# Hybrid attention, S5 and PEER block on one core: gather steps handed out between the dense blocks, GELU as one ScalarE operation

## The chip, the core and the metric

The kernel runs on one core of a Trainium2 chip. The metric is the device time of one execution in microseconds (us), the median of several runs. The engines are TensorE (PE; PEld is its weight load), VectorE (DVE), ScalarE (ACT), GpSimd (POOL), which issues the indirect gathers here, and SyncE (SP), which issues most other transfers. Sixteen DMA engines move the data.

## The reference

One block of a diffusion backbone works on 1024 latent tokens of width 1024 with 256 context tokens: attention and a state-space branch, merged by gates and projected, then PEER retrieval, then the output. All is in float32. The part that matters here is the last one, PEER: for each token eight heads choose 16 of 16384 single-neuron experts each, so 128 rows of `peer_u` and 128 rows of `peer_v`.

```python
def retrieve(xb):                       # one block of 128 tokens
    ...                                 # top-k of product keys -> experts, top_s
    g = jax.nn.softmax(top_s, axis=-1).astype(xb.dtype)
    act = jax.nn.gelu(jnp.einsum('thkd,td->thk', u_tab[experts], xb))
    return jnp.einsum('thk,thkd->td', g * act, v_tab[experts])
```

`jax.nn.gelu` is the tanh form: 0.5 x (1 + tanh(c2 x (1 + c1 x^2))).

## The kernel before

The 1024 tokens are eight tiles of 128. They go through the front part (attention, gates, projection, routing) in four groups: tile 0; 1 and 2; 3, 4 and 5; 6 and 7. `route` chooses the experts of a group. The retrieval is then done in two ways.

**By gathers** (tiles 0, 1, and 6, 7, the list `VEC`). `score` takes 128 steps per tile: in a step GpSimd gathers one row of `peer_u` per token (tile `ub`, 128 x 1024, L1274), and DVE multiplies it with the tile's input and sums to one dot product (L1278). `weighted` then applies the GELU and the gate to the 128 x 128 dot products and takes another 128 steps: a gather of `peer_v` rows (`vb`, L1316) and one DVE step that adds the weighted row to the sum `f` (L1319). All gathered rows share six buffers. `retrieve` interleaves the two: the weighted steps of one tile stand between the scoring steps of the next. For tiles 6 and 7 that is 512 gathers.

**Over all experts** (tiles 2 to 5, the list `DENSE`, 512 tokens at once). `dense` goes through the 16384 experts in 128 blocks of 128, two to a turn of its loop. A block loads its part of `peer_u` (transposed) and `peer_v` and splits each into a high and a low part (`u`, `v`: a cast on ACT and a subtraction on DVE of 1024 columns, L232 and L233). 24 matmuls of 512 columns (L1233 to L1235) give the dot products of all 512 tokens in one bank, `turn`. The GELU and a product with `gt`, which holds each token's gate for the experts of the block and zero elsewhere (spread out earlier from `pl` by `spread`), follow in 128 x 512 tiles `x` and `act`. The result is split into `kpe_h` and `kpe_l`, and 24 more matmuls (L1194 to L1196) add high and low products to the sums `fd` of four tiles by two halves. Seven of those eight sums have a bank of their own. The last, the "aside", has none: its three matmuls write to `turn`, from where ACT copies them (`more`, L1201) and DVE adds them to `rest` (L1202). In the code the values of a block come after the `turn` matmuls of the next (`late`).

The program is emitted in one order of code, with priorities, and a scheduler then fixes the order of the instructions of each engine at build time; each engine runs its own list in that order. The last lines of `block_kernel` are where the two ways meet: the first pairs of blocks are emitted between steps of the last group's routing, then `retrieve(VEC)` emits all 512 gather steps, and after it come the remaining pairs of blocks. What is emitted earlier has the better place where both are ready. The GELU of a block before is

```python
                S.copy(x, turn)
                S.activation(w, x, func=AF.Square, scale=math.sqrt(GC1))
                V.scalar_tensor_tensor(w, w, 1.0, x, op0=ADD, op1=MUL)
                xc = x.rearrange("p (c t) -> p c t", t=CHUNK)
                V.tensor_tensor(xc, xc, gt[:, :, 2 * (p % GTP) + c, :], op=MUL)
                S.activation(w, w, func=AF.Tanh, scale=GC2)
                V.scalar_tensor_tensor(w, w, 1.0, x, op0=ADD, op1=MUL)
```

where `S` is ACT and `V` is DVE. These are L1238 to L1244.

## Time and profile before

| what | value |
| --- | --- |
| time, median of 3 runs | 3889.87 us (3882.73 to 3898.87) |
| profiled execution | 3890.37 us, of which the profile's span is 3888.6 us |
| PE busy, share of the span | 3431.8 us, 88% |
| DVE busy | 3037.1 us, 78% |
| ACT busy | 1645.2 us, 42% |
| POOL busy | 1443.5 us, 37% |
| moved by DMA | 1032.55 MB, 266 GB/s on the mean |
| mean granted clock of PE | 0.936 |

The span is one execution as the hardware profiler saw it. Busy times are unions of what the engine's instructions cover; matmuls are pipelined, so the duration of one overlaps the next, and the pace is better read from how many of them fall in a stretch. The granted clock is the share of TensorE's full clock that it got. A wait is put down to the engine and line that released it last. Shares over the whole span mix the front part with the stage over all experts; the stretches below are cut from that stage.

### The profile page before, as it was taken

How to read it: one execution, taken by the hardware profiler on the slowest of the kernel's cores; microseconds unless marked ns; L12 is line 12 of the kernel's file. 1: busy time of each engine (PE TensorE's matmuls, PEld its weight loads, DVE VectorE, ACT ScalarE, POOL GpSimd, SP SyncE). 2: the span in 40 equal slices, each digit the busy share in tenths (PEclk: the TensorE clock that was granted, in tenths of full speed). 3: DMA queues.
4: the chain of work that ended last, by engine and by line, in shares of the span. 5: the costliest groups of instructions: out<-in, count | busy, mean ns of one | idle time of the engine just before them, and what ended most of it. 6: DMA issues, size and time to landing. Idle time of an engine off the chain costs nothing.

```text
span 3888.6 us, 55690 instructions
## 1 busy us (share of the span) xinstructions
PE 3431.8 (88%) x20022; PEld 2769.1 (71%) x20022; DVE 3037.1 (78%) x7128; ACT 1645.2 (42%) x3216; POOL 1443.5 (37%) x1254
## 2 busy tenths in 40 slices
PE   5978888879779899799999798899889999999997
PEld 3745577878656688576687687677667777777885
DVE  7368656775898776889566688999999999998556
ACT  2223363441323564133498953334333344444442
POOL 5045300040554633543522102765666653442000
PEclk7988899999889999899999899899999999999998
DMA  8742375494897899978877655999999998897331
GB/s 281 223 83 71 128 268 193 159 358 167 312 347 271 313 346 339 341 280 285 309 286 310 263 179 197 353 352 336 343 350 359 345 349 297 311 336 273 115 124 71
DMA packets 348725, 1032.55 MB, mean 266 GB/s; under 512 B 46592, under 2 KB 142080, under 8 KB 322592
## 3 DMA queue, kind: packets, MB, share of 16 engines
q0 software_dynamic: 147456, 536.94, 37.8%
q1 hardware_dynamic: 164032, 462.20, 33.6%
q10 hardware_dynamic: 36960, 29.86, 2.4%
q8 instruction: 157, 2.57, 0.3%
q14 instruction: 120, 0.98, 0.1%
HBM read 961.27 MB, written 67.62 MB: 265 GB/s over the span
## 4 chain that ended last, share of the span: by engine, by line
PE 43%; issue 12%; DVE 12%; DMA 8%; ACT 5%; POOL 5%; another core or an unknown queue 0%; SPq 0%; DVEq 0%; POOLq 0%; ACTq 0%
DMA ub<-in_peer_u,ei 4%; PE turn L1234 4%; PE turn L1233 4%; POOL ub L1274 4%; PE turn L1235 4%; DVE ub L1278 4%; PE fd L1195 4%; PE fd L1196 4%; PE fd L1194 3%; PE acc L1354 2%; PE pe L1151 2%; PE pqr L1065 2%; PE po L808 2%; ACT first L1147 1%; DMA vb<-in_peer_v,eiT 1%
## 5 line engine op out<-in xcount | busy, mean ns | idle before, releaser
L1274 POOL DMA_INDIRECT ub<-in_peer_u,ei x512 | 649.2, 1268 | 1130.8 <-DVE ub L1278 350.7
L1278 DVE SCALAR_TENSOR_TENSOR ub<-ub,h 128x1024 f32<-128x1024 f32 x512 | 617.2, 1220 | 64.3 <-DMA ub<-in_peer_u,ei 55.0
L1316 POOL DMA_INDIRECT vb<-in_peer_v,ei x256 | 327.4, 1279 | 316.6 <-DVE f L1319 257.3
L1349 POOL DMA_INDIRECT vb<-in_peer_v,eiT x256 | 281.3, 1099 | 415.3 <-PE acc L1354 318.4
L1195 PE MATMUL fd<-v,kpe_l 128*128 128x512 f32 x891 | 366.8, 412 | 44.4 <-DVE kpe_l L233 44.3
L1233 PE MATMUL turn<-hh,u 128*128 128x512 f32 x1024 | 401.1, 392 | 0.2 <-ACT x L1238 0.2
L1234 PE MATMUL turn<-hh,u 128*128 128x512 f32 x1024 | 400.7, 391 | 0.1
L1235 PE MATMUL turn<-hl,u 128*128 128x512 f32 x1024 | 399.3, 390 | 0.0
L1194 PE MATMUL fd<-v,kpe_h 128*128 128x512 f32 x891 | 341.7, 404 | 35.5 <-ACT kpe_h L232 35.3
L1196 PE MATMUL fd<-v,kpe_h 128*128 128x512 f32 x891 | 359.8, 404 | 0.0
L1319 DVE SCALAR_TENSOR_TENSOR f<-vb,zz,f 128x1024 f32<-128x1024 f32 x254 | 325.3, 1281 | 4.9 <-DMA vb<-in_peer_v,ei 3.8
L233 DVE TENSOR_TENSOR u<-w,u 128x1024 fp32r<-128x1024 f32 x128 | 157.9, 1234 | 116.2 <-ACT u L232 112.7
L1195 PEld LDWEIGHTS fd<-v,kpe_l 128*128 128x128 f32 x891 | 173.5, 195 | 91.4 <-DVE kpe_l L233 52.6
L1194 PEld LDWEIGHTS fd<-v,kpe_h 128*128 128x128 f32 x891 | 170.6, 193 | 84.9 <-ACT kpe_h L232 43.3
L1233 PEld LDWEIGHTS turn<-hh,u 128*128 128x128 f32 x1024 | 192.2, 188 | 43.5 <-ACT x L1238 0.4
L1235 PEld LDWEIGHTS turn<-hl,u 128*128 128x128 f32 x1024 | 192.3, 188 | 41.9
L1234 PEld LDWEIGHTS turn<-hh,u 128*128 128x128 f32 x1024 | 192.2, 188 | 40.8 <-DVE u L233 0.5
L1238 ACT COPY x<-turn 128x512 f32<-128x512 f32 x128 | 75.0, 586 | 316.4 <-PE turn L1235 316.3
L232 ACT CAST v<-w 128x1024 fp32r<-128x1024 f32 x128 | 134.6, 1052 | 167.7 <-PE fd L1195 163.1
L1354 PE MATMUL acc<-vb,diag 128*32 128x256 f32 x2048 | 163.1, 399 | 46.7 <-DMA vb<-in_peer_v,eiT 42.2
L1148 DVE TENSOR_SCALAR second<-iota,pl 128x128 f32<-128x128 f32 x512 | 141.5, 350 | 79.4 <-PE pe L1151 65.6
L1196 PEld LDWEIGHTS fd<-v,kpe_h 128*128 128x128 f32 x891 | 173.3, 194 | 40.8
(422 smaller groups left out, 8623.7 us busy)
## 6 DMA issues: line engine op xcount, KB each, us to landing
w<-in_peer_uT SPq DMA_DIRECT2D x64, 1024.0 KB
w<-in_peer_v SPq DMA_DIRECT2D x64, 1024.0 KB
w<-in_peer_wq SPq DMA_DIRECT2D x32, 1024.0 KB
gT_d<-stage SPq DMA_DIRECT2D x16, 2048.0 KB
gt<-gT_d SPq DMA_DIRECT2D x32, 1024.0 KB
vh<-v_d SPq DMA_DIRECT2D x32, 640.0 KB
w<-k_d SPq DMA_DIRECT2D x32, 640.0 KB
w<-in_w_mod_b SPq DMA_DIRECT2D x16, 1024.0 KB
```

What stands on the lines that cost most here:

```text
L1194: PE.matmul(o, ah[:, ts], vh[:, cs], start=first, stop=False)
L1195: PE.matmul(o, al[:, ts], vh[:, cs], start=False, stop=False)
L1196: return PE.matmul(o, ah[:, ts], vl[:, cs], start=False, stop=final)
L1233: PE.matmul(turn, uh[:, k, :], hh[:, k, :], start=(k == 0), stop=False)
L1234: PE.matmul(turn, ul[:, k, :], hh[:, k, :], start=False, stop=False)
L1235: PE.matmul(turn, uh[:, k, :], hl[:, k, :], start=False, stop=(k == 7))
L1274: GP.indirect_dma_start(out=ub, out_offset=None, in_=a["peer_u"], in_offset=bass.IndirectOffsetOnAxis(ap=ei[:, s:s + 1], axis=0))
L1278: V.scalar_tensor_tensor(ub, ub, 1.0, h2, op0=MUL, op1=MUL, accum_out=dots[:, s:s + 1])
L1316: GP.indirect_dma_start(out=vb, out_offset=None, in_=a["peer_v"], in_offset=bass.IndirectOffsetOnAxis(ap=ei[:, s:s + 1], axis=0))
L1319: V.scalar_tensor_tensor(f, vb, z[:, s:s + 1], f, op0=MUL, op1=ADD)
L1349: GP.indirect_dma_start(out=vb, out_offset=None, in_=a["peer_v"], in_offset=bass.IndirectOffsetOnAxis(ap=eiT[:, t:t + 1], axis=0))
L1354: PE.matmul(acc[d // 2][o:o + 32, 256 * (d % 2):256 * (d % 2) + 256], dg[:, q, jj, :], vb[:, d * 256:(d + 1) * 256], start=False, stop=Fal ...
```

## The change

Three things change. In a block of `dense`, one ACT operation, `Gelu_apprx_tanh`, reads the bank `turn` and writes `act`, which now has two buffers; the copy `x`, the square, the tanh and two of the three DVE steps are gone. The factor 0.5 that the gates `pl` carried is gone too, since this GELU has it. In `weighted`, the tiles 6 and 7 use the same ACT operation; tiles 0 and 1 keep the old form. And `retrieve` is a generator now: the remaining pairs of blocks are emitted first in each turn of a loop, and eight steps of `retrieve(VEC)` after each pair, until the steps run out.

```diff
-                    S.mul(pl[:, 2], pt[:, 1, :], 0.5)
+                    S.copy(pl[:, 2], pt[:, 1, :])
...
-                x = N.tile([128, ntok], F32, tag="x", name="x")
-                w = N.tile([128, ntok], F32, tag="act", name="act")
-                S.copy(x, turn)
-                S.activation(w, x, func=AF.Square, scale=math.sqrt(GC1))
-                V.scalar_tensor_tensor(w, w, 1.0, x, op0=ADD, op1=MUL)
-                xc = x.rearrange("p (c t) -> p c t", t=CHUNK)
-                V.tensor_tensor(xc, xc, gt[:, :, 2 * (p % GTP) + c, :], op=MUL)
-                S.activation(w, w, func=AF.Tanh, scale=GC2)
-                V.scalar_tensor_tensor(w, w, 1.0, x, op0=ADD, op1=MUL)
+                w = N.tile([128, ntok], F32, tag="act", bufs=2, name="act")
+                S.activation(w, turn, func=AF.Gelu_apprx_tanh)
+                wc = w.rearrange("p (c t) -> p c t", t=CHUNK)
+                V.tensor_tensor(wc, wc, gt[:, :, 2 * (p % GTP) + c, :], op=MUL)
...
             for s, _ in enumerate(score(l, ei, dots)):
                 if n and s % n == 0:
                     next(before, None)
+                yield
             for _ in before:
-                pass
+                yield
             before = weighted(l, ei, eiT, g, dots)
         for _ in before:
-            pass
+            yield
...
+        if l in VEC:
+            S.activation(z, dots, func=AF.Gelu_apprx_tanh)
+            V.tensor_tensor(z, z, g, op=MUL)
+        else:
...
-    retrieve(VEC)
-    with tc.high_priority(offset=PDENSE):
-        for _ in tokens:
-            pass
+    beside = retrieve(VEC)
+    for _ in tokens:
+        for _ in range(PACE):
+            next(beside, None)
+    for _ in beside:
+        pass
```

`PACE` is 8, `tokens` is the generator of `dense` (one pair of blocks a step). Below, lines after the change are a few numbers lower or higher: the scoring step L1278 is L1273, the product with the gates L1242 is L1239, and the new GELU is L1237.

**DVE in the scoring of tile 6**, one block from gate product to gate product. Before:

```order
L1244 SCALAR_TENSOR_TENSOR act<-act,x 128x512
L1278 SCALAR_TENSOR_TENSOR ub,dots<-ub,h_22240 128x1024 x2
L233 TENSOR_TENSOR v<-w,v 128x1024
L233 TENSOR_TENSOR kpe_l<-act,kpe_h 128x512
L1278 SCALAR_TENSOR_TENSOR ub,dots<-ub,h_22240 128x1024 x4
L233 TENSOR_TENSOR u<-w,u 128x1024
L1240 SCALAR_TENSOR_TENSOR act<-act,x 128x512
L1202 TENSOR_TENSOR rest<-rest,more 128x512
L1278 SCALAR_TENSOR_TENSOR ub,dots<-ub,h_22240 128x1024 x2
L1242 TENSOR_TENSOR x<-x,gt 128x512
```

After, in the same stretch:

```order
L233 TENSOR_TENSOR u<-w,u 128x1024
L1273 SCALAR_TENSOR_TENSOR ub,dots<-ub,h_22343 128x1024
L1202 TENSOR_TENSOR rest<-rest,more 128x512
L233 TENSOR_TENSOR kpe_l<-act,kpe_h 128x512
L1273 SCALAR_TENSOR_TENSOR ub,dots<-ub,h_22343 128x1024 x2
L233 TENSOR_TENSOR v<-w,v 128x1024
L1273 SCALAR_TENSOR_TENSOR ub,dots<-ub,h_22343 128x1024 x2
L1239 TENSOR_TENSOR act<-act,gt 128x512
```

Two of the five steps of 512 columns are gone from the block, and five scoring steps stand in it where eight stood; over the whole stretch the mean was 6.7 and is 4.8. Counted over the lists, the 512 gather steps of tiles 6 and 7 lay on blocks 9 to 102 and now lie on blocks 9 to 119 (blocks are counted from 0).

**PE between two `turn` groups**, where the aside writes to `turn`. Before, as in 53 of the 127 blocks:

```order
L1235 MATMUL turn<-hl,u 128x512
L1194 MATMUL fd<-v,kpe_h 128x512 x2
L1194 MATMUL turn<-v,kpe_h 128x512
L1195 MATMUL fd<-v,kpe_l 128x512
L1196 MATMUL fd<-v,kpe_h 128x512
```

After, as in 57 of them, the end of one block's values and the `turn` group of the next:

```order
L1194 MATMUL fd<-v,kpe_h 128x512
L1195 MATMUL fd<-v,kpe_l 128x512
L1196 MATMUL fd<-v,kpe_h 128x512
L1194 MATMUL fd<-v,kpe_h 128x512 x2
L1233 MATMUL turn<-hh,u 128x512
...
L1235 MATMUL turn<-hl,u 128x512
L1195 MATMUL fd<-v,kpe_l 128x512
L1196 MATMUL fd<-v,kpe_h 128x512
L1195 MATMUL fd<-v,kpe_l 128x512
L1196 MATMUL fd<-v,kpe_h 128x512
L1194 MATMUL turn<-v,kpe_h 128x512
```

In these blocks the first two products with `kpe_h` moved ahead of the next block's `turn` group, and four matmuls instead of two stand between that group and the aside; in most of the other blocks six do, as in most of the others before.

**ACT beside the last routing**, after the change (`g` is the softmax of a tile's gates; `qh` and `sc` are copies of the routing). Before, the same place has no table load:

```order
L1069 COPY qh<-pqr 128x256
L1038 ACTIVATE g<-g 128x64
L1237 ACT_TABLE_LOAD
L1237 ACTIVATE act<-turn 128x512
L232 CAST u<-w 128x1024
L1074 COPY sc<-pz 128x256
L1038 ACT_TABLE_LOAD
L1038 ACTIVATE g<-g 128x64
```

Seven such loads are new, all in this stretch; the lists have ten after and three before.

## Rows read from the trace of the kernel before

**Rows 1.** Page, busy tenths in 40 slices: TensorE, and its granted clock in tenths.
```profile
PE   5978888879779899799999798899889999999997
...
PEclk7988899999889999899999899899999999999998
```

**Rows 2.** Stretches: us; PE, PEld, DVE, ACT, POOL busy (instructions); clock, DMA share, GB/s.
```profile
2390.00:3842.00 1452.00, 1362.99 (x5689) 1082.77 (x5688) 1270.42 (x1662) 582.41 (x832) 678.14 (x511) 0.97 0.82 295
3580.00:3842.00 262.00, 262.00 (x1136) 212.95 (x1135) 133.39 (x178) 113.56 (x165) 0.00 (x0) 1.00 0.35 117
2390.00:2660.00 270.00, 232.57 (x933) 182.34 (x932) 256.05 (x404) 95.82 (x137) 185.55 (x130) 0.92 0.94 343
2745.00:3130.00 385.00, 341.38 (x1376) 266.27 (x1375) 372.44 (x510) 140.71 (x201) 254.20 (x187) 0.95 0.95 350
3270.00:3550.00 280.00, 276.59 (x1185) 220.99 (x1183) 268.55 (x285) 121.83 (x173) 133.03 (x112) 1.00 0.92 327
```

**Rows 3.** Waits of TensorE from 2390 to 2660 us: us in total, times, longest.
```profile
PE fd L1194 <- ACT kpe_h L232: 20.2, 6, 11.0
PE fd L1195 <- DVE kpe_l L233: 16.1, 8, 3.5
```

**Rows 4.** The same from 2745 to 3130 us.
```profile
PE fd L1195 <- DVE kpe_l L233: 26.2, 14, 4.0
PE fd L1194 <- ACT kpe_h L232: 15.1, 8, 3.3
```

**Rows 5.** VectorE in order of time near 2600 us: start, us, instruction.
```profile
2600.53 0.68 DVE L1244 SCALAR_TENSOR_TENSOR act<-act,x 128x512 f32<-128x512 f32 x1
2601.13 1.21 DVE L233 TENSOR_TENSOR v<-w,v 128x1024 fp32r<-128x1024 f32 x1
2602.27 1.21 DVE L1278 SCALAR_TENSOR_TENSOR ub<-ub,h 128x1024 f32<-128x1024 f32 x1
...
2603.41 0.68 DVE L233 TENSOR_TENSOR kpe_l<-act,kpe_h 128x512 fp32r<-128x512 f32 x1
```

**Rows 6.** The same near 3350 us, weighted steps.
```profile
3350.78 1.27 DVE L1319 SCALAR_TENSOR_TENSOR f<-vb,zz,f 128x1024 f32<-128x1024 f32 x1
3351.97 0.68 DVE L1244 SCALAR_TENSOR_TENSOR act<-act,x 128x512 f32<-128x512 f32 x1
```

**Rows 7.** VectorE's groups from 2745 to 3130 us: xcount, busy us, mean ns.
```profile
L1278 DVE SCALAR_TENSOR_TENSOR ub<-ub,h 128x1024 f32<-128x1024 f32 x123 | 148.2, 1219 | 5.9 <-DMA ub<-in_peer_u,ei 5.6 <-issue 0.2
L1319 DVE SCALAR_TENSOR_TENSOR f<-vb,zz,f 128x1024 f32<-128x1024 f32 x64 | 82.2, 1285 | 3.9 <-DMA vb<-in_peer_v,ei 3.5 <-DVE rest L1202 0.3
```

**Rows 8.** ScalarE's groups by form, whole span: xcount, busy us, mean ns.
```profile
L871 ACT ACTIVATE P<-pS,mb 128x512 f32<-128x512 f32 x128 | 87.0, 686 | 108.2 <-DVE mb L866 95.9 <-DVE mb L865 8.0 <-DVE eiT L1108 2.2
L1239 ACT ACTIVATE act<-x 128x512 f32<-128x512 f32 x128 | 81.0, 633 | 48.6 <-DVE kpe_l L233 48.5
...
L232 ACT CAST kpe_h<-act 128x512 fp32r<-128x512 f32 x128 | 79.3, 620 | 165.3 <-DVE act L1244 165.2
...
L1238 ACT COPY x<-turn 128x512 f32<-128x512 f32 x128 | 75.0, 586 | 316.4 <-PE turn L1235 316.3
...
L629 ACT ACT_TABLE_LOAD x1 | 1.3, 1283 | 0.4 <-ACT vt L698 0.4
```

**Rows 9.** Waits of TensorE from 3300 to 3540 us.
```profile
PE turn L1194 <- ACT x L1238: 2.9, 11, 0.3
```

**Rows 10.** DMA from 2390 to 3580 us: packets, MB, share; one issue row.
```profile
q0 software_dynamic: 73728, 268.47, 61.5%
q1 hardware_dynamic: 69431, 128.42, 30.8%
...
w<-in_peer_v SPq DMA_DIRECT2D x47, 1024.0 KB
```

**Rows 11.** Waits of VectorE from 2390 to 3580 us.
```profile
DVE ub L1278 <- DMA ub<-in_peer_u,ei: 15.5, 21, 1.8
...
DVE f L1319 <- DMA vb<-in_peer_v,ei: 3.8, 6, 1.0
```

More of the change, by code (lines that the diff above doesn't have):

```diff
@@ L69 @@
 PRIO = (0, 1500, 1500, 3000, 2000)
-PDENSE = 0
+PACE = 8
 RAT = 3
@@ L1305, in weighted @@
         z = pp.tile([128, 128], F32, tag="zz", name="zz")
-        V.tensor_tensor(z, dots, dots, op=MUL)
-        V.tensor_scalar(z, z, GC1, 1.0, op0=MUL, op1=ADD)
-        V.tensor_tensor(z, z, dots, op=MUL)
-        S.activation(z, z, func=AF.Tanh, scale=GC2)
-        V.scalar_tensor_tensor(z, z, 1.0, dots, op0=ADD, op1=MUL)
-        V.scalar_tensor_tensor(z, z, 0.5, g, op0=MUL, op1=MUL)
+        if l in VEC:
+            S.activation(z, dots, func=AF.Gelu_apprx_tanh)
+            V.tensor_tensor(z, z, g, op=MUL)
+        else:
+            V.tensor_tensor(z, dots, dots, op=MUL)
+            V.tensor_scalar(z, z, GC1, 1.0, op0=MUL, op1=ADD)
+            V.tensor_tensor(z, z, dots, op=MUL)
+            S.activation(z, z, func=AF.Tanh, scale=GC2)
+            V.scalar_tensor_tensor(z, z, 1.0, dots, op0=ADD, op1=MUL)
+            V.scalar_tensor_tensor(z, z, 0.5, g, op0=MUL, op1=MUL)
         if l in VEC:
@@ L1468, in block_kernel @@
         if gi == RAT:
-            retrieve([l for l in range(NL) if l not in DENSE + VEC])
+            for _ in retrieve([l for l in range(NL) if l not in DENSE + VEC]):
+                pass
     with tc.high_priority(offset=PRIO[-1]):
@@ L1484, in block_kernel @@
     turns[1] = 1
-    retrieve(VEC)
-    with tc.high_priority(offset=PDENSE):
-        for _ in tokens:
-            pass
+    beside = retrieve(VEC)
[3 more added lines that the diff above has]
+    for _ in beside:
+        pass
     psum.release()
```

## The prediction

> **What bounds the kernel now.** I read the page's slices first. The change acts only where the stage over all experts runs, from slice 23 or 24 on (a slice is 97.2 us), since the order of every engine is the same up to its first block. There TensorE (PE) is busy 8 or 9 tenths of nearly every slice and its clock is at or near full, with dips on the way [rows 1]. So the question is how much of that stage is PE work and how much is PE waiting.
>
> The table of stretches answers it. A block of the stage is 48 matmuls of 512 columns. From 3580 to 3842 us no gather runs any more, PE is busy for all 262 us at clock 1.00 and does 1136 matmuls: 262 / 1136 = 0.2306 us each, 11.07 us for a block [rows 2]. I take that as PE's own pace. From 2390 to 3842 us it did 5689 matmuls, which at that pace take 1312 us; they took 1452. So **140 us** of this stage are lost, and nothing that speeds up the other engines can win back more. Where: 270 - 933 x 0.2306 = 55 us from 2390 to 2660, 385 - 1376 x 0.2306 = 68 us from 2745 to 3130, and only 280 - 1185 x 0.2306 = 7 us from 3270 to 3550 [rows 2]. In the two bad stretches the granted clock was 0.92 and 0.95 on the mean, so part of the loss is the clock that fell after PE had idled; the idle itself is 270 - 233 = 37 and 385 - 341 = 44 us.
>
> The waits of PE name the releaser: fd L1194 and L1195 wait for kpe_h and kpe_l, the two halves of the activations, 20.2 + 16.1 us and 15.1 + 26.2 us [rows 3, 4]. These come out of the GELU chain, most of which stands in the queue of VectorE (DVE), and DVE is busy 256 of 270 and 372 of 385 us there [rows 2].
>
> Is it DVE's own work? The spacing of starts in the timeline gives what an instruction takes from the queue: 0.60 us for 512 columns, 1.14 for a split of 1024 or for one scoring step, 1.19 for one weighted step [rows 5, 6]. A block of before has two splits of 1024 and five of 512 columns (L1240, L1242, L1244, kpe_l, rest): 2 x 1.14 + 5 x 0.60 = 5.28 us. From 2745 to 3130 us that is 1376 / 48 = 28.7 blocks x 5.28 = 151, plus 123 x 1.14 = 140 for scoring and 64 x 1.19 = 76 for weighting [rows 7], together 367 of 385 us. So DVE set the pace there, at 13.4 us a block. From 3270 to 3550 us 112 gathers fell on 24.7 blocks, 4.5 a block, DVE needed 5.28 + 4.5 x 1.19 = 10.7 us, less than 11.07, and PE was bound by itself. The bound is thus **DVE where more than about 4.8 gathers fall on a block, and PE elsewhere**.
>
> **The change part by part.**
>
> *The GELU.* Per block it takes L1240 and L1244 off DVE (2 x 0.60 us) and the copy, the square and the tanh off ScalarE (ACT; rows of 586 and 633 ns [rows 8]) and adds one ACT operation from PSUM. DVE's share of a block falls from 5.28 to 4.08 us. The new operation isn't in the trace; its bounds are the PSUM copy of the same tile, 586 ns, and the exponential from PSUM of the same size, 686 ns [rows 8]; I take 640, nearest to the tanh of 633. Either way it is hidden: ACT has over half its time free. It also holds the bank "turn" as the copy did, so the next user, the aside's first L1194, must wait for it. In the order of before two matmuls often stand ahead of that one and it waits, at most 0.3 us a time [rows 9]; in the new order at least four stand ahead in nearly every block (0.92 us), which covers 0.69 and a semaphore. If the operation took over 1 us that cover would be gone.
>
> *Table loads.* The new order has seven more ACT_TABLE_LOADs, all beside the route of the last group, where GELU and the Exp of L1038 alternate; after that none. One took 1283 ns [rows 8]: 9.0 us on ACT, spread over the blocks in which PE has the route's matmuls to do as well. Between 0 (all covered) and 9 us I take 4, because a load just ahead of a GELU also delays the release of "turn".
> The Trainium skill (ScalarE: Activation LUTs, "Table sets: the hidden batching unit") says to batch activations by table set rather than by function, which speaks against this change, and prices a load at some 2.7 us; by that the term would be up to 19 us. This case's row has about half that price, so the row decides, and the built order shows that only seven alternations are left.
>
> *The gather steps.* All 512 of the last two token tiles stay; they move. Before, they had the better place in the queue and sat at 6.7 and 6.5 a block in the scoring stretches, ending 25 blocks before the end. Now they lie over blocks 9 to 119, 4.6 a block, densest 4.8 (blocks 9 to 35). DVE then needs 4.08 + 4.6 x 1.17 = 9.5 us of each 11.07, 85%; in the densest 9.6. So DVE no longer sets the pace and **the waits for kpe_h and kpe_l should go**. With PE not idling I also expect the clock rows to stay at 1.00, as they do from 3270 on.
>
> *What is late next: DMA.* The gathers' queue took 61.5% of 1190 us for 511 gathers, 1.43 us each, and the loads' queue 30.8% for 47 pairs of blocks, 3.9 us a block [rows 2, 10]. The new mix asks for 4.6 x 1.43 + 3.9 = 10.5 us in 11.07, a share of 0.95; the densest part 10.8, 0.97. A share of 0.92 went together with PE at full pace (3270 to 3550), and 0.95 was held for 385 us [rows 2], with DVE waiting for gathers only 15.5 + 3.8 us in the whole stretch to 3580 [rows 11]. So it fits, narrowly. If 0.95 is the most that it holds, the 27 dense blocks take 10.8 / 0.95 = 11.35 us, 8 us in all. Each gather on GpSimd's queue waits only for a free row buffer; the loads stand on SP's queue in the old sequence, the loads of the two tile ends now later in it.
>
> *The rest.* The 0.5 that leaves the copy of the gates costs nothing (same copy, same size). The tail after 3842 us is PE and the settling of four tiles, unchanged.
>
> **Sum**, against the profiled run (3890.4 us, span 3888.6; the median of the runs is 3889.9, so no correction): -140 if PE never waits. Added back: 4 for table loads, 8 for DMA, and 12 for small waits: at 4.5 gathers a block the loss was 7 in 280 us, 2.5%, and since the aside's part of it should go I take 1% of the 111 x 11.07 = 1229 us. 3890.4 - 140 + 24 = **3774 us**. Its own range is 3750 (no loss at all) to 3788.
>
> **The rivals.**
>
> *DMA becomes the bound.* For it: the share of 0.95 is the highest that any long stretch shows, and gathers now run nearly to the end, so no slack is left behind them. Against: DVE's waits for gathers were small even there. If only 0.92 or 0.90 can be used, blocks take (1.43 x gathers + 3.9) / share: over the four parts of the gather stretch (4.81, 4.57, 4.63 and 4.44 a block, 27, 7, 41 and 36 blocks) that adds 37 or 65 us to 3890.4 - 140 + 4: **3791 to 3819 us**.
>
> *A new wait for kpe_h.* In some 57 blocks the new order puts the first two L1194 of a block's values ahead of the next block's "turn" matmuls, so kpe_h is wanted 24 x 0.2306 = 5.5 us after "turn" ends, not 11. The chain is 0.69 (GELU) + 0.60 (gate product) + 0.62 (kpe_h [rows 8]) = 1.9 us, plus what DVE has in hand: three scoring steps still fit (5.3), a fourth or a gather that is late (longest 1.8 us [rows 11]) does not. At 1 to 2 us for each of 57 blocks, on top of the forecast: **3831 to 3888 us**, the upper end no change.
>
> *Slower: the gathers set the end.* All gathers share six row buffers, and one late gather holds everything behind it on DVE, the gate product and the splits included. If thinner spacing made a gather cost more than 2.7 us, the last would land after 2390 + 512 x 2.7 = 3772, then 8 blocks (89) and the tail (47) give 3908, and from there on the kernel is slower. At 2.9 us it is **4010 us**. Against: a gather cost 385 / 187 = 2.06 us when pushed and 2.5 us when the order spaced it [rows 2]; the plan asks for 2.4.
>
> *It doesn't do what it says.* If the GELU operation took 1.5 us or more from PSUM, the aside would wait some 0.7 us in each block, 85 us: about **3860 us**. No row comes near that duration.
>
> **How the numbers follow.** Forecast (3750 to 3788) 0.60; DMA as the bound 0.22; the new wait for kpe_h 0.08 (a quarter of it within 0.5% of now, which is about what a measurement of this kernel can tell from no change); slower 0.05; a slow GELU 0.05 (half of it within 0.5%). Faster by over 0.5%, that is below 3870: 0.60 + 0.22 + 0.06 + 0.02 = 0.90; within: 0.05; slower: 0.05. The range for 8 in 10 runs from 3748 to 3822: it takes in the forecast and the DMA case to its dearer end.
>
> **What would show it.** Right: in the stretches of the gathers some 173 matmuls in 40 us, clock 1.00, DVE about 85% busy, no wait of PE for kpe_h or kpe_l above a few us in total, a GELU row of about 0.64 us, DMA at 0.93 to 0.96, gathers ending some 90 us before the last block. Wrong: DVE idle in front of the scoring and weighted steps, released by the gathers' DMA (DMA bound); PE idle before fd L1194 released by kpe_h although DVE has time free (new wait); PE idle before turn L1194 in every block (slow GELU). The prediction fails altogether if PE's pace of 0.2306 us, taken where DMA ran at a share of 0.35, can't be held beside gathers.

## The result and the profile after

The changed kernel takes 3759.27 us (median of 4 runs, 3758.54 to 3767.63) beside 3888.99 us for the kernel before on the same chip (4 runs): a ratio of 0.9669, 95% interval 0.9651 to 0.9687. The profiled execution took 3758.8 us, its span 3757.0: 131.6 us less than the profiled one of before.

The page's slices of the kernel after, TensorE and its granted clock, to be read beside [rows 1]:

```profile
PE   5968888979779889879989879999999999999997
...
PEclk7978999989889989989999989999999999999998
```

The first 24 slices are much like before; from slice 25 (a slice is 93.9 us now) PE is at 9 in all but the last, and the clock with it. The stretches of the stage, with the columns of [rows 2]:

```profile
2390.00:2430.00 40.00, 37.89 (x162) 29.81 (x161) 35.33 (x59) 12.93 (x18) 25.05 (x18) 1.00 0.83 296
2430.00:2510.00 80.00, 78.10 (x331) 62.84 (x330) 70.56 (x107) 24.62 (x34) 50.19 (x37) 0.98 0.98 367
2510.00:2670.00 160.00, 160.00 (x694) 129.47 (x693) 140.09 (x209) 54.00 (x75) 91.78 (x68) 1.00 0.94 336
2745.00:3130.00 385.00, 385.00 (x1668) 312.07 (x1667) 335.38 (x434) 126.73 (x172) 215.87 (x161) 1.00 0.94 341
3160.00:3540.00 380.00, 380.00 (x1646) 306.95 (x1645) 337.93 (x365) 124.22 (x171) 215.89 (x152) 1.00 0.93 335
```

Where before did 1376 matmuls in the 385 us from 2745 on, after does 1668, one every 0.2308 us; DVE fell from 372 to 335 us busy (87%), and DMA from 0.95 to 0.94 although the stage goes faster. Of the waits of PE, those on kpe_h [rows 3, 4] are gone and those on kpe_l nearly so. From 2390 to 3700 us all that is left of PE's waits is:

```profile
PE fd L1195 <- DVE kpe_l L233: 3.6, 3, 1.7
PE turn L1194 <- ACT act L1237: 0.4, 2, 0.2
```

The GELU and the table loads, ScalarE's groups by form (xcount, busy us, mean ns, idle before), beside [rows 8]:

```profile
L1237 ACT ACTIVATE act<-turn 128x512 f32<-128x512 f32 x128 | 76.6, 598 | 588.0 <-PE turn L1235 587.9
...
L1237 ACT ACT_TABLE_LOAD x4 | 5.1, 1283 | 0.1
...
L1038 ACT ACT_TABLE_LOAD x3 | 3.8, 1283 | 0.1
```

For the comparisons below two measures are worked out from the order in time of ScalarE and VectorE, the same way for each kernel. **Block 9 to 127** is the time from the start of block 9's first ScalarE operation on `turn` to that of block 127; 118 blocks at 11.07 us are 1306 us. It leaves out the front part, which differs between profiled runs (block 9 began at 2384 us in one and at 2416 in another, with the same work ahead of it). **The chain** of a block runs from that same start to the end of its kpe_l. Both are from one profiled execution of each kernel. The six kernels in which gather steps and blocks are tied to each other (explained below) take 45 us from the start of block 127 to their end, before and after 39; those 6 us go with the ties.

| kernel | gather steps per block while scoring | ratio to before (95%) | block 9 to 127, us | chain in blocks 42 to 83: mean (longest), us |
| --- | --- | --- | --- | --- |
| before | 6.5 to 6.7 | 1 | 1446.5 | 11.7 (16.9) |
| after | 4.6 to 4.8 | 0.9669 (0.9651 to 0.9687) | 1315.7 | 4.8 (6.0) |
| new GELU alone | as after | 0.9659 (0.9612 to 0.9706) | 1313.5 | 4.8 (6.0) |
| hand-out alone | as before | 1.001 (0.9988 to 1.0033) | 1450.5 | 11.7 (17.3) |
| old GELU, spread steps | as after | 0.9987 (0.9966 to 1.0008) | 1436.0 | 13.1 (16.9) |
| the same, steps behind kpe_l | as after | 0.9887 (0.9864 to 0.991) | 1391.4 | 11.2 (16.6) |
| new GELU, dense steps | as before | 0.9963 (0.9946 to 0.998) | 1430.5 | 9.7 (22.3) |
| the same, steps behind kpe_l | as before | 0.9989 (0.9971 to 1.0006) | 1440.5 | 9.6 (18.8) |
| the same, half rows | as before | 0.9823 (0.9798 to 0.9847) | 1368.0 | 7.7 (15.2) |
| after + 2 DVE operations beside | 5.5 to 5.6 | 0.9792 (0.977 to 0.9815) | 1369.4 | 10.4 (16.8) |
| after + 4 ACT operations in the chain | 4.6 to 4.9 | 0.9662 (0.9645 to 0.968) | 1323.0 | 7.5 (9.8) |
| after + 8 ACT operations in the chain | 4.7 to 5.1 | 0.9717 (0.9694 to 0.974) | 1332.2 | 10.4 (11.8) |
| after + a write of 0.5 MB per pair | as after | 0.9812 (0.9778 to 0.9846) | 1365.8 | 9.0 (19.7) |

So before lost 140 us against 1306 between these two blocks, and after loses 9. Seven of the nine lie in blocks 10 to 12, the first behind the last routing, whose chains take 10.6 to 15.6 us.

### The profile page after: what moved, and what is told of

Read it like the earlier page. It is cut to its first block, busy times and chain, and to the rows that moved or that the text cites. A ratio compares the mean times of both kernels' runs of the same rounds, so it can differ in the third digit from the quotient of the medians.

```text
span 3757.0 us, 54909 instructions
## 1 busy us (share of the span) xinstructions
PE 3376.1 (90%) x20022; PEld 2741.5 (73%) x20022; DVE 2889.2 (77%) x6864; ACT 1496.5 (40%) x2967; POOL 1477.3 (39%) x1254
## 4 chain that ended last, share of the span: by engine, by line
PE 56%; DVE 9%; issue 7%; DMA 5%; ACT 4%; POOL 2%; SPq 0%; DVEq 0%; ACTq 0%; POOLq 0%
PE turn L1233 6%; PE turn L1234 6%; PE turn L1235 6%; PE fd L1194 5%; PE fd L1195 5%; PE fd L1196 5%; DMA ub<-in_peer_u,ei 2%; PE pqr L1065 2%; DVE ub L1273 2%; PE acc L1354 2%; PE pe L1151 2%; DMA vb<-in_peer_v,eiT 2%; PE po L808 2%; PE po L953 1%; POOL ub L1269 1%
## 5 line engine op out<-in xcount | busy, mean ns | idle before, releaser
L1269 POOL DMA_INDIRECT ub<-in_peer_u,ei x512 | 639.6, 1249 | 1221.7 <-DVE ub L1273 446.8
L1273 DVE SCALAR_TENSOR_TENSOR ub<-ub,h 128x1024 f32<-128x1024 f32 x512 | 617.0, 1219 | 52.4 <-DMA ub<-in_peer_u,ei 46.5
L1316 POOL DMA_INDIRECT vb<-in_peer_v,ei x256 | 363.4, 1420 | 266.3 <-DVE f L1319 203.6
L1195 PE MATMUL fd<-v,kpe_l 128*128 128x512 f32 x891 | 353.5, 397 | 3.6 <-DVE kpe_l L233 3.6
L1196 PE MATMUL fd<-v,kpe_h 128*128 128x512 f32 x891 | 351.1, 394 | 0.0
L1194 PE MATMUL fd<-v,kpe_h 128*128 128x512 f32 x891 | 341.5, 397 | 0.0
L1237 ACT ACTIVATE act<-turn 128x512 f32<-128x512 f32 x128 | 76.6, 598 | 588.0 <-PE turn L1235 587.9
L1196 PEld LDWEIGHTS fd<-v,kpe_h 128*128 128x128 f32 x891 | 167.6, 188 | 41.5
L1194 PEld LDWEIGHTS fd<-v,kpe_h 128*128 128x128 f32 x891 | 167.3, 188 | 40.7
L233 DVE TENSOR_TENSOR v<-w,v 128x1024 fp32r<-128x1024 f32 x128 | 156.6, 1223 | 43.4 <-ACT v L232 42.7
```

What stands on the lines that cost most here:

```text
L1194: PE.matmul(o, ah[:, ts], vh[:, cs], start=first, stop=False)
L1195: PE.matmul(o, al[:, ts], vh[:, cs], start=False, stop=False)
L1196: return PE.matmul(o, ah[:, ts], vl[:, cs], start=False, stop=final)
L1269: GP.indirect_dma_start(out=ub, out_offset=None, in_=a["peer_u"], in_offset=bass.IndirectOffsetOnAxis(ap=ei[:, s:s + 1], axis=0))
L1273: V.scalar_tensor_tensor(ub, ub, 1.0, h2, op0=MUL, op1=MUL, accum_out=dots[:, s:s + 1])
L1316: GP.indirect_dma_start(out=vb, out_offset=None, in_=a["peer_v"], in_offset=bass.IndirectOffsetOnAxis(ap=ei[:, s:s + 1], axis=0))
```

## The experiments

### Which part of the change did it

Two kernels do one part each. The GELU alone, from the kernel after:

```diff
-    beside = retrieve(VEC)
+    for _ in retrieve(VEC):
+        pass
     for _ in tokens:
-        for _ in range(PACE):
-            next(beside, None)
-    for _ in beside:
         pass
```

> The changed kernel without its hand-out: all gather steps are written out ahead of the blocks again, as before, and only the GELU is new. Theory A (the new GELU does everything: less VectorE and ScalarE work in a block, and the scheduler, which places instructions by its own costs, puts the gather steps between the blocks by itself at 4.6 per block): same time as the changed kernel, 3759 us, ratio to before 0.967 within 0.002. Theory B (the prediction's own wording: the hand-out is what thins the gather steps from 6.5 to 4.6 per block): the scoring stretches stay dense, VectorE's account there is 4.08 + 6.6 x 1.16 = 11.7 us per block against TensorE's 11.07, so about 49 blocks x 0.65 = 32 us are lost again: 3790 us or more, ratio 0.975 or more.

The hand-out alone, from the kernel before:

```diff
-    retrieve(VEC)
-    with tc.high_priority(offset=PDENSE):
-        for _ in tokens:
-            pass
+    beside = retrieve(VEC)
+    for _ in tokens:
+        for _ in range(PACE):
+            next(beside, None)
+    for _ in beside:
+        pass
```

> The kernel before with the hand-out alone (eight gather steps written out after every two blocks), its old GELU of six operations kept. Theory A: the written order decides nothing, 3889 us, ratio 1.000 within 0.002, with the turns on kpe_h and kpe_l of the kernel before (20 to 26 us and 15 us in the two scoring stretches). Theory B: the spacing becomes 4.6 per block, VectorE's account 5.28 + 4.6 x 1.16 = 10.6 us per block is under TensorE's 11.07, and most of the 130 us is gained: 3770 to 3800 us, ratio 0.97 to 0.977.

Measured: 3756.87 us (0.9659, 0.9612 to 0.9706) and 3892.35 us (1.001, 0.9988 to 1.0033). Theory A holds in both. The stretch from 2745 to 3130 us, first of the GELU alone:

```profile
2745.00:3130.00 385.00, 385.00 (x1669) 312.04 (x1668) 335.02 (x433) 127.92 (x174) 214.89 (x160) 1.00 0.94 340
```

and of the hand-out alone:

```profile
2745.00:3130.00 385.00, 340.39 (x1370) 266.12 (x1369) 369.31 (x506) 138.94 (x198) 255.65 (x185) 0.94 0.95 348
```

The one is the kernel after, the other the kernel before. The built orders say why: on each of the five engines the list of the GELU alone is that of the kernel after, instruction for instruction, and the list of the hand-out alone that of before. The traces show it too: in both pairs every operation of PE, VectorE, ScalarE and GpSimd stands at the same place. I read it so that the scheduler places a step where its own reckoning finds it ready and the engine free, and that eight steps per turn of the loop never held it back; the lists show only that they changed nothing. So the whole gain comes with the GELU part of the edit, and the thinner spacing of the steps, which I had put down to the hand-out, came with it too. That part also holds the second buffer of `act` and the shorter `weighted`; the three weren't built apart.

### Less work in a block, or fewer steps in a block?

The new GELU changes two things in the built order: less stands in a block, and fewer gather steps stand between two blocks. To take them apart, the gather steps were tied to blocks: by the counts of the kernel after with the old GELU, and by the counts of before with the new one (`PLAN` holds the counts, `share` draws that many steps ahead of each product; `block` marks the product, `step` the last gather step). The first:

```diff
-                V.tensor_tensor(xc, xc, gt[:, :, 2 * (p % GTP) + c, :], op=MUL)
+                share()
+                marks["block"] = V.tensor_tensor(xc, xc, gt[:, :, 2 * (p % GTP) + c, :], op=MUL)
...
-            with tc.issue_after(marks[held[-1]].ins) if held else nullcontext():
+            behind = marks["block"] if l in VEC else marks[held[-1]] if held else None
+            with tc.issue_after(behind.ins) if behind else nullcontext():
```

> The old GELU of six operations, but each gather step tied behind the block that it stands behind in the changed kernel, so that the steps per block (4.6 over blocks 9 to 121) are the changed kernel's. Theory C (what counts is how much stands between two blocks, gathers and GELU together; per block VectorE 5.28 + 4.6 x 1.16 = 10.6 us, the 16 DMA engines 4.6 x 1.43 + 3.9 = 10.5 us, both under 11.07): the stage is nearly at TensorE's pace, 3765 to 3800 us, ratio 0.968 to 0.977. Theory D (the old chain of six operations over two engines, from turn to kpe_l, is itself what TensorE waited for in the scoring stretches, whatever stands between the blocks): the waits stay, 3850 to 3890 us, ratio 0.99 to 1.00.

The second:

```diff
-                V.tensor_tensor(wc, wc, gt[:, :, 2 * (p % GTP) + c, :], op=MUL)
+                share()
+                with tc.issue_after(marks["step"].ins) if "step" in marks else nullcontext():
+                    V.tensor_tensor(wc, wc, gt[:, :, 2 * (p % GTP) + c, :], op=MUL)
```

> The new GELU, but each block's product with the gates tied behind the gather step that it stands behind in the kernel before: 6.5 to 6.7 steps per block in the scoring stretches, 4.5 in the weighted ones, done by block 101. Theory C1 (VectorE was the bound of the scoring stretches): its account is 4.08 + 6.6 x 1.16 = 11.7 us per block instead of 13.3, so of before's 2.3 us per block over the pace 0.65 stay on some 49 blocks: +32 us, about 3790 us, ratio 0.975. Theory C2 (the transfers were: 6.6 x 1.43 + 3.9 = 13.3 us of the 16 DMA engines per block, with the GELU no part of it): the scoring stretches stay as slow as before, +110 us, about 3870 us, ratio 0.995, with VectorE's waits for the gathered rows in place of TensorE's cause. In between would say that both are near the bound.

Measured: 3887.18 us (0.9987, 0.9966 to 1.0008) and 3879.36 us (0.9963, 0.9946 to 0.998). Built in this way, the one half alone gives none of the gain that can be measured, the other a tenth. The same stretch in both, old GELU with spread steps first:

```profile
2745.00:3130.00 385.00, 363.68 (x1498) 287.33 (x1497) 338.21 (x437) 154.99 (x220) 198.03 (x144) 0.96 0.86 303
```

```profile
2745.00:3130.00 385.00, 346.43 (x1398) 272.29 (x1396) 337.91 (x450) 107.50 (x144) 249.62 (x185) 0.94 0.95 347
```

In the first neither DVE (88%) nor the transfers (0.86) are full, and yet PE is held. In the second DVE is at 88% too, about as in the kernel after, but the transfers stand at 0.95. So VectorE's load on the mean, on which the prediction rested, can't be what holds either of them. Where the first loses is seen in VectorE's order of time (start, us, instruction; the block's copy from `turn` began at 2863.96 on ACT):

```profile
2863.96 0.59 ACT L1246 COPY x<-turn 128x512 f32<-128x512 f32 x1 [1.74 <-PE turn L1243]
```

```profile
2866.67 0.68 DVE L1248 SCALAR_TENSOR_TENSOR act<-act,x 128x512 f32<-128x512 f32 x1
...
2867.88 0.68 DVE L1251 TENSOR_TENSOR x<-x,gt 128x512 f32<-128x512 f32 x1
2868.48 1.22 DVE L1289 SCALAR_TENSOR_TENSOR ub<-ub,h 128x1024 f32<-128x1024 f32 x1
...
2869.62 1.28 DVE L1338 SCALAR_TENSOR_TENSOR f<-vb,zz,f 128x1024 f32<-128x1024 f32 x1
2870.82 1.22 DVE L1289 SCALAR_TENSOR_TENSOR ub<-ub,h 128x1024 f32<-128x1024 f32 x1
...
2871.97 1.22 DVE L1289 SCALAR_TENSOR_TENSOR ub<-ub,h 128x1024 f32<-128x1024 f32 x1
...
2873.11 0.69 DVE L1253 SCALAR_TENSOR_TENSOR act<-act,x 128x512 f32<-128x512 f32 x1
...
2876.05 0.72 DVE L241 TENSOR_TENSOR kpe_l<-act,kpe_h 128x512 fp32r<-128x512 f32 x1
```

The chain takes 2876.77 - 2863.96 = 12.8 us, 4.6 of them for four gather steps in a row between its two halves, where the tie to the product puts them. In the kernel after, a block that starts at the same time:

```profile
2863.92 0.60 ACT L1237 ACTIVATE act<-turn 128x512 f32<-128x512 f32 x1 [4.67 <-PE turn L1235]
```

```profile
2864.55 0.69 DVE L1239 TENSOR_TENSOR act<-act,gt 128x512 f32<-128x512 f32 x1 [1.42 <-issue]
...
2867.44 0.68 DVE L233 TENSOR_TENSOR kpe_l<-act,kpe_h 128x512 fp32r<-128x512 f32 x1
```

4.2 us. This gave a new theory: the chain of a block has about one block time, 11.07 us, until PE wants its end, and a longer one sets the pace by itself (theory E below).

### The chain's place in the queue, and the bytes

The old GELU with spread steps again, but the steps tied behind the block's kpe_l and not its product, so that they don't gather in the middle of the chain:

```diff
-                marks["block"] = V.tensor_tensor(xc, xc, gt[:, :, 2 * (p % GTP) + c, :], op=MUL)
+                V.tensor_tensor(xc, xc, gt[:, :, 2 * (p % GTP) + c, :], op=MUL)
...
-                split(ah, al, w)
+                marks["block"] = split(ah, al, w)
```

> The old GELU and the changed kernel's gather steps per block, as in the run on the spread alone, but each step is tied behind the block's last VectorE operation (the subtraction into kpe_l) instead of behind its product in the middle of the chain; on VectorE the steps now stand singly between the chain's operations, not four in a row ahead of its second half. Theory E (what TensorE waits for is the latency from a block's last turn matmul to its kpe_l, which has one block, 11.07 us, of cover; in the run on the spread alone it measured 12.5 us because of the steps in a row, in the changed kernel 4.7 us): the chain is the 8.2 us that the old one takes with no gather beside it plus one or two steps of 1.2 us, under 11.07, so nearly TensorE's pace: 3765 to 3795 us, ratio 0.968 to 0.976. Theory D (the old chain of six operations is too long in any order): 3850 to 3890 us.

Measured: 3836.14 us (0.9887, 0.9864 to 0.991), between the two theories. With the same instructions, counts and transfers as the spread steps tied to the product, block 9 to 127 fell from 1436 to 1391 us: the order within the block alone is worth 45 us, and that much theory E has right. But the chain came down to 11.2 us only, not to the 9.4 to 10.6 that I reckoned, and 14 of the 42 blocks from 42 to 83 are still over 11.07. With the old GELU and 4.6 steps DVE has 5.28 + 4.6 x 1.17 = 10.7 us of work in 11.07, so each operation of the chain mostly finds something ahead of it.

The same tie for the dense steps with the new GELU, both ties together (products behind the steps, steps behind the kpe_l ahead):

> The new GELU and the kernel before's gather steps per block (6.6 in the scoring stretches), as in the run on the density alone, but each step is tied behind the kpe_l of the block ahead, so that the steps are at work while the chain is not. Theory E or C1 (there it was the chain's latency, 13.4 us, or VectorE's work, 4.08 + 6.6 x 1.16 = 11.7 us per block): the stretches run at 11.7 us per block, 3785 to 3800 us, ratio 0.973 to 0.977. Theory C2 (the transfers bound a dense stretch: 6.6 x 1.43 + 3.9 = 13.3 us of the 16 DMA engines per block): no better than the run on the density alone, 3865 to 3880 us, ratio 0.994 to 0.998.

and this kernel with half the bytes:

```diff
-            GP.indirect_dma_start(out=ub, out_offset=None, in_=a["peer_u"],
+            GP.indirect_dma_start(out=ub[:, 0:512], out_offset=None,
+                                  in_=a["peer_u"].rearrange("n (h d) -> (n h) d", h=2),
...
+                twice = ub[:, 0:512].unsqueeze(1).to_broadcast([128, 2, 512])
-                mark = V.scalar_tensor_tensor(ub, ub, 1.0, h2, op0=MUL, op1=MUL, accum_out=dots[:, s:s + 1])
+                mark = V.scalar_tensor_tensor(scrap, twice, 1.0, h2, op0=MUL, op1=MUL, accum_out=dots[:, s:s + 1])
```

(shortened: `scrap` is the other half of the buffer, `h2` is viewed as two halves, and `vb` is done in the same way).

> The same, with half of each gathered row only (512 of 1024 columns, from another row of the table; VectorE goes over the half twice, so that its work stays): the gathers of this stage move half the bytes and their sums are not the reference's. Transfers per block in the scoring stretches 6.6 x 0.72 + 3.9 = 8.7 us. Theory C2: the stretches go from 13.3 to VectorE's 11.7 us per block, 49 blocks x 1.6 = 78 us and more faster than the run with whole rows, about 3790 us. Theory C1 or E: same time as the run with whole rows within 10 us.

Measured: 3875.0 us (0.9989, 0.9971 to 1.0006) with whole rows and 3816.23 us (0.9823, 0.9798 to 0.9847) with half rows. Whole rows, then half rows:

```profile
2745.00:3130.00 385.00, 332.08 (x1338) 263.35 (x1339) 329.07 (x439) 105.07 (x141) 238.56 (x179) 0.92 0.94 342
```

```profile
2745.00:3130.00 385.00, 368.14 (x1551) 294.40 (x1550) 373.68 (x489) 121.46 (x162) 288.69 (x203) 0.98 0.76 251
```

A better place for the steps gave nothing, half the bytes gave 59 us, and 72 between block 9 and 127. With half rows the transfers fall to 0.76, and DVE rises to 374 us, 97%, and is now what is full, at 385 x 48 / 1551 = 11.9 us a block for the 11.7 of its account. This is nearly the pace and the gain that C2 forecast (11.7 us a block, 78 us), but it doesn't show C2, for half the bytes changed the orders too: 295 of VectorE's 6352 operations in the two traces stand at another place, and 45 of ScalarE's 2967. PE's largest wait in the stretch, whole rows and then half rows, is:

```profile
PE fd L1202 <- ACT kpe_h L240: 51.7, 13, 8.2
```

```profile
PE fd L1202 <- ACT kpe_h L240: 14.3, 5, 4.0
```

The tie of the product is behind it. The product of a block stands behind all of the block's gather steps, up to 11 by the plan, and in some blocks ScalarE's list then has the cast into kpe_h behind the GELU of the next block. With whole rows that is so in 20 blocks from block 9 on, with half rows in 9, in the run with dense steps and that tie alone in 16; in the kernels whose product is not tied, before and after among them, in none. PE then waits in the block that follows. Of the 134 us by which block 9 to 127 lies over TensorE's pace with whole rows, 125 fall in those 20 following blocks; with half rows 49 of 62 in 9, and with one tie 109 of 124 in 16. So most of what these kernels lose goes with an order that before and after don't have. For a part of the bytes themselves speaks that VectorE's waits for gathered rows in the stretch, with whole rows

```profile
DVE ub L1285 <- DMA ub<-in_peer_u,ei: 14.1, 11, 2.5
...
DVE f L1336 <- DMA vb<-in_peer_v,ei: 12.0, 8, 2.3
```

are 3.6 and 1.8 us with half rows. How much of the 72 us is the bytes' and how much the order's stays open, and with it whether the transfers held the kernel before.

### VectorE's load without the chain, and the chain without the load

The kernel after with two more operations of 512 columns on VectorE, off the chain:

```diff
                 V.tensor_tensor(wc, wc, gt[:, :, 2 * (p % GTP) + c, :], op=MUL)
+                for _ in range(2):
+                    V.tensor_tensor(gt[:, :, 2 * (p % GTP) + c, :], gt[:, :, 2 * (p % GTP) + c, :], wc, op=MUL)
```

> The changed kernel with two more VectorE operations of 128x512 in each block that are no part of the chain (they multiply the block's gates by act once more, in place, where nobody reads them again): VectorE's work per block is the kernel before's, 5.44 us, the chain stays the new one. The scheduler then places 5.6 steps per block in the scoring stretches (blocks 10 to 32 and 39 to 75) of itself. Theory C1 (VectorE's load): 5.44 + 5.6 x 1.16 = 11.9 us per block, 60 blocks x 0.85 = 50 us: 3800 to 3815 us, ratio 0.977 to 0.981. Theory E (only the chain's latency counts, which stays near 5 to 7 us): 3759 to 3770 us. That the load alone makes the kernel before's time: 3880 us or more.

and with four and eight copies on ScalarE, in the chain:

```diff
                 V.tensor_tensor(wc, wc, gt[:, :, 2 * (p % GTP) + c, :], op=MUL)
+                for _ in range(4):
+                    S.copy(w, w)
```

> The changed kernel with four more ScalarE copies of 128x512 in place (about 0.6 us each) in the chain, between the product with the gates and the split into kpe_h and kpe_l: the chain becomes 4.7 + 2.4 = 7 to 8 us long, VectorE's work and the gather steps per block (4.6 to 4.8) stay. Theory E (a chain costs nothing until it reaches the 11.07 us of a block): no loss, 3757 to 3765 us, ratio 0.966 to 0.969. Theory F (each us on the chain costs TensorE directly, or the casts behind the copies on ScalarE come late): up to 2.4 us per block on 112 blocks, 4020 us; half of that already 3890 us.

> The same with eight copies: the chain becomes 9.5 to 10.5 us, as long as in the old GELU with single gather steps between its operations (10.5 to 11.2 us there, at 3836 us), while VectorE's work per block stays at 4.08 us. Theory E: still under 11.07 us in most blocks, 3760 to 3785 us. Theory C1 (that kernel's 3836 us was the chain's length, not VectorE's load of 96%): about 3830 us here too. ScalarE's own account, 3.6 + 8 x 0.6 = 8.4 us per block, is no bound.

Measured: 3803.56 us (0.9792, 0.977 to 0.9815), 3764.95 us (0.9662, 0.9645 to 0.968) and 3789.39 us (0.9717, 0.9694 to 0.974). The stretch in the three, in this order:

```profile
2745.00:3130.00 385.00, 365.51 (x1517) 288.77 (x1517) 370.79 (x507) 117.26 (x158) 255.10 (x175) 0.97 0.94 344
```

```profile
2745.00:3130.00 385.00, 385.00 (x1668) 312.88 (x1667) 335.47 (x435) 210.72 (x313) 219.95 (x161) 1.00 0.94 339
```

```profile
2745.00:3130.00 385.00, 383.03 (x1650) 308.75 (x1648) 337.91 (x433) 292.68 (x448) 231.53 (x162) 1.00 0.94 337
```

The load on VectorE costs 54 us of the 131 between block 9 and 127: DVE is full again, at 371 of 385 us, and what the chain does in its queue follows from that (10.4 us on the mean, though nothing was added to it). That is C1's number. It also moved the steps: with this load the scheduler put 5.5 to 5.6 of them in a block by itself, where the longer chains hardly moved its spacing (4.6 to 5.1). So VectorE's load in the scheduler's reckoning makes about half of the step from 4.7 to 6.6; where the other half comes from wasn't tested.

The chain's length costs nothing at 7.5 us in that stretch (1668 matmuls, as in the kernel after), and little at 10.4: 1650, with 6 of the 42 blocks over 11.07. From block 9 to 127 the four copies add 7 us, all of it in blocks 9 to 12, and the eight copies 16.5, of which 9 lie there. So a chain that stays under one block of cover is nearly free, as theory E has it, and F is out. The kernel before agrees: from 3270 to 3550 us its chain is 10.9 us on the mean, 11.2 at the longest, and PE waits for neither kpe_h nor kpe_l there. That a chain over 11.07 us sets the pace by itself isn't shown, as none was run with VectorE free. The eight copies were run on another chip than after; beside the kernel before on the same chips the ratios are 0.9717 and 0.9669. E's upper end, 3785, was missed by 4 us on a chip on which before took 3896.65. In the profiled runs block 9 began 17 us later than after's; whether the copies beside the routing did that, or the scatter of the front part, stays open.

### How far the transfers are from being the next bound

A first try, a copy of 0.5 MB from memory to memory for each pair of blocks:

```diff
+            SY.dma_start(spare_d[p], a["peer_v"][256 * p:256 * p + 128])
```

> The changed kernel with a copy of 0.5 MB from memory to memory for each pair of blocks (128 rows of peer_v into a spare buffer that nobody reads), on SyncE's queue. At 3.9 us of the 16 DMA engines for 1.05 MB of stream, the copy adds about 0.95 us per block: the account becomes 10.5 + 0.95 = 11.45 us against TensorE's 11.07. If the transfers stand as near to being the next bound as their account says: 0.4 us on some 112 blocks, 3795 to 3830 us, ratio 0.976 to 0.985. If the share of 0.94 has more room in it than that: 3757 to 3765 us.

Measured: 3861.89 us (0.9914, 0.9895 to 0.9932), and it says nothing on the stage. The copies depend on nothing, so the scheduler issued them all at the start; the issues from 0 to 800 us have

```profile
spare_d<-in_peer_v SPq DMA_DIRECT2D x64, 512.0 KB
```

and the 102 us were lost there: block 9 began at 2504.5 us, and block 9 to 127 took 1317.6 us as in the kernel after. The second try ties the transfer to the block's own data, and the steps to the counts of the kernel after:

```diff
+            SY.dma_start(spare_d[p], vt[:, 0, :])
```

> The changed kernel with its gather steps tied between the same blocks as there (same steps per block), and for each pair of blocks one more transfer of 0.5 MB, which writes the first half of the pair's loaded peer_v out to a spare buffer that nobody reads; it stands on SyncE's queue just ahead of the next pair's loads, so that it can't leave the stage as the copies did. In the run with the copies all 64 left for the first 800 us of the program, and the stage kept its pace. Account of the 16 DMA engines per block: 10.5 + 0.95 = 11.45 us against TensorE's 11.07. If the transfers are the next bound: 0.4 us and more on some 112 blocks, 3795 to 3840 us, ratio 0.976 to 0.987. If there is more room in them: 3757 to 3770 us.

Measured: 3807.4 us (0.9812, 0.9778 to 0.9846), in the range of the first case.

```profile
2745.00:3130.00 385.00, 374.41 (x1595) 299.93 (x1593) 317.49 (x413) 124.52 (x166) 199.04 (x153) 0.99 0.96 346
```

DVE has less in hand than in the kernel after (317 of 385 us), the transfers are at 0.96, and block 9 to 127 is 50 us longer, for 0.38 x 118 = 45 by the account. But the trace shows another cause for most of it. Order of time on VectorE, ScalarE and PE near block 53:

```profile
2894.97 0.68 DVE L1251 TENSOR_TENSOR act<-act,gt 128x512 f32<-128x512 f32 x1
```

```profile
2896.11 0.60 ACT L1247 ACTIVATE act<-turn 128x512 f32<-128x512 f32 x1 [4.66 <-PE turn L1245]
2896.61 1.04 ACT L241 CAST u<-w 128x1024 fp32r<-128x1024 f32 x1
2897.54 0.62 ACT L241 CAST kpe_h<-act 128x512 fp32r<-128x512 f32 x1
```

```profile
2898.22 0.73 PE L1203 MATMUL fd<-v,kpe_h 128*128 128x512 f32 x2 [2.14 <-ACT kpe_h L241]
```

The product of block 52 is done at 2895.65 and ScalarE is idle, but its list has the cast of kpe_h behind the GELU of block 53, which waits for PE's `turn` matmuls. PE then waits 2.14 us. Nine blocks have this order, as in the runs above whose product is tied, and no block of the kernel after. In each of the nine that follow PE waits 2.1 to 5.4 us for kpe_h, and they lie 3.1 to 10.3 us over 11.07, together 46 of the 60 us by which the run lies over TensorE's pace. The other 109 blocks are 14 us over, where the kernel after is 9 over in all. So the agreement with the account is luck: the greater part of the 50 us goes with an order that only the kernels with a tied product have. The ties alone, without the write, weren't run. How much room the transfers have in the kernel after stays open; its account (10.5 of 11.07 us) is all there is.

## Why the prediction was right

The time, 3759, lies 15 us under the forecast of 3774 and in its own range (3750 to 3788); none of the rivals came. Step by step:

- **140 us of loss, a floor of 3750, a pace of 0.2306 us that holds beside gathers.** Right. 1668 matmuls in 385 us are 0.2308 us each, at a DMA share of 0.94. That was the condition on which all the rest hung.
- **The GELU: 640 ns between 586 and 686, hidden.** 598 ns, and the aside waited 0.4 us in all from 2390 to 3700 us, for 2.9 in 240 us before [rows 9].
- **Table loads: 4 us.** All seven are there (4 and 3 in the groups above), at 1283 ns. PE's only waits for the GELU beside the routing, 2260 to 2400 us, are 1.4 + 1.2 us, against 0.9 for the copy there before, so about 1.7 us.
- **DVE 85% busy, the waits on kpe_h and kpe_l gone, the clock at 1.00, DMA 0.93 to 0.96.** 87%, 3.6 us, 1.00, 0.93 to 0.94 (0.98 and 0.98 for clock and DMA in the 80 us from 2430 on).
- **What was put back: 24 us. Over-sized.** 140 - 131.6 leaves 8. About 1.7 came for the table loads. From 2390 to 2510 us 162 + 331 matmuls stand where 520 fit, 6 us: 4.0 of them are PE's waits for kpe_l and the GELU, the rest stands beside a granted clock of 0.98. The larger ones, 1.5 and 1.7 us, come behind a scoring step ahead of block 10's product that waited 3.7 us for its rows (first row below the list). So one late gather came in place of the 8 us that were set for DMA, as a share of 0.95 over 27 dense blocks; from 2510 us on PE kept its pace beside 0.93 to 0.94. The 12 for small waits were taken from a stretch of before in which PE waited for the aside alone, from 3270 to 3550 us (second row below the list). The prediction itself expected that wait to go, and it went; the 1% of the whole stage that it still set had no wait behind it.
- **The gather steps move because of the hand-out. Wrong.** The hand-out moves nothing. I took the two parts' common result for the work of the part that bore the name. The forecast was right in spite of it, since it rested on the counts of the built order and not on their cause.
- **VectorE is the bound of the kernel before where more than 4.8 gathers fall on a block. Right as far as the runs go, with one rival open.** VectorE was 97% busy at 13.4 us a block, and with two operations put back it was 96% busy at 385 x 48 / 1517 = 12.2, for 11.9 by its account; in both the steps are untied. Two more stood at the same place before: the transfers at 6.6 x 1.43 + 3.9 = 13.3 by their account, and the chain, 13.2 us on the mean from 2745 to 3130. The chain without VectorE's load cost little as far as it was lengthened (10.4 us). For the transfers nothing is settled, since every run with dense steps and a light VectorE is a tied one. The prediction has the rows for the transfers' account [rows 10], and used them for the new mix but not for the old. That each half undone alone (old GELU with spread steps, new GELU with dense steps) fell back to the time of before, or with the better tie to 0.9887, is in part the ties' doing.

The step that waited, VectorE after:

```profile
2418.74 1.23 DVE L1273 SCALAR_TENSOR_TENSOR ub<-ub,h 128x1024 f32<-128x1024 f32 x1 [3.74 <-DMA ub<-in_peer_u,ei]
```

and all of PE's waits before, from 3270 to 3550 us:

```profile
PE turn L1194 <- ACT x L1238: 3.4, 13, 0.3
```

The scheduler fixed the order of before at 6.5 steps a block. With 1.2 us less on VectorE, and a shorter chain, it fixed the order at 4.6, where DVE (9.5 us), the transfers (10.5 by their account) and the chain (4.8) are all under PE's 11.07. Which of the three alone would have been enough isn't shown.

Of the rivals, **DMA as the bound** did not come in the kernel after; the run with more transfers doesn't show how near it is. The **new wait for kpe_h** did not come either: from 2390 to 3700 us PE waited for kpe_h nowhere. For the **slower** case the gathers would have had to end after 3772 us; block 119, the last with gather steps, began at 3629.

## What to carry to other kernels

Before an edit is credited, build each part of it alone and compare the orders: a hint to a scheduler may change nothing, and a cheaper instruction may move everything around it. Where several engines work beside a bound one, write out each one's account per turn of the loop, transfers and the latency of the dependent chain included, for the kernel before as well as for the one after. An experiment that ties instructions to hold a count fixed makes an order of its own: before its time is read, look for waits that the untied kernels don't have, and build the tie alone. In an engine that works in order, what matters of a short operation in a chain is what stands ahead of it: four steps of 1.2 us between two halves of a chain were 4.6 of its 12.8 us.

## What the runs showed of the hardware

The GELU from PSUM (598 ns) is 12 ns above the plain copy of the same tile from PSUM (586) and under the tanh from SBUF (633, [rows 8]). So this function cost what moving the tile costs; the exponential from PSUM, with a second operand, stands at 686 [rows 8].

A table load cost little more than its 1283 ns. In ScalarE's order of time after, the neighbours of one stand within 0.02 us on both sides:

```profile
2368.01 0.26 ACT L1038 ACTIVATE g<-g 128x64 f32<-128x64 f32 x1 [2.50 <-DVE g L1037]
2368.29 1.28 ACT L1237 ACT_TABLE_LOAD   x1
2369.58 0.60 ACT L1237 ACTIVATE act<-turn 128x512 f32<-128x512 f32 x1
```

The Trainium skill (ScalarE: Activation LUTs, "What ACT_TABLE_LOAD costs") has the same 1283 ns for the load, and adds a drain of about 1380 ns for each switch; no row here shows that second part.

The transfers: the 385 us from 2745 on moved 341 GB/s in the kernel after and 350 in the kernel before, and 80 us of the run with the write moved more,

```profile
3390.00:3470.00 80.00, 79.56 (x342) 63.53 (x341) 68.81 (x68) 26.08 (x35) 44.25 (x33) 1.00 1.01 375
```

with PE a little short of its pace (342 for 347). The Trainium skill (DMA: Bandwidth & Descriptors, "Specifications") gives about 358 GB/s per core as the limit of the memory; the long stretches lie under it, the 375 of that one stretch above. Half a row did not cost half: over 2390 to 3540 us the gathers' queue with whole and with half rows (packets, MB, share):

```profile
q0 software_dynamic: 72399, 263.61, 62.0%
```

```profile
q0 software_dynamic: 40960, 134.25, 36.2%
```

That is 1.42 us of the 16 engines for a gather of 128 rows of 4 KB (0.62 x 1150 us for 503 of them) and 0.81 us for 2 KB (0.362 x 1150 for 512), where I had set 0.72.

The idle of PE cost more than itself: in the run with dense steps and the new GELU, from 2745 to 3130 us, 1398 matmuls at full pace would be 322 us, so 63 are lost; 39 of them are idle, and the other 24 stand beside a granted clock of 0.94.
